# A gated product streamed through three SBUF slots: its DMA issues moved from SyncE to GpSimd, one packet per engine

## The chip, the cores and the metric

The kernel runs on one core of a Trainium2 chip. The metric is the device time of one execution in microseconds (us). Engines are named as in the profile: DVE is VectorE, ACT is ScalarE, POOL is GpSimd, SP is SyncE; a "q" behind a name (SPq) is the engine's instruction queue, in which waits and DMA issues are recorded. A core has 16 DMA engines, which move data between the chip's memory and SBUF.

## The reference

```python
def setup_inputs():
    return {"x": np.random.randn(8192, 8192).astype(np.float32)}

def reference(x):
    a, b = np.split(x, 2, axis=-1)
    silu_b = b / (1 + np.exp(-b))
    return a * silu_b
```

Each row of x has 8,192 floats. The first half is multiplied by the SiLU of the second half, which gives 4,096 floats. 268.4 MB are read and 134.2 MB written.

## The kernel before

The 8,192 rows are taken in 16 groups of 512. A group gives each of the 128 partitions four rows that follow one another in memory (R = 4). One group is loaded in two halves, `load(g, 0)` and `load(g, 1)`: two of the four rows, 64 KB per partition and 8.4 MB in all. The result of a group is four half rows per partition, again 64 KB, and is written by one `store(g)`. So there are 32 loads and 16 stores of the same size, 48 transfers in all.

There are three slots in SBUF of 64 KB per partition. For each group one slot is `keep` (it takes the first half and later holds the whole result) and one is `thru` (it takes the second half, which is read out of it). `swiglu(g, second, k0, k1)` works on rows k0 to k1 of a half: ScalarE replaces b by its SiLU in place (L72), VectorE multiplies a by it and writes the product into the `keep` slot (L74). The first half is done with one call of 2 x 4,096 elements per partition, the second with two calls of 4,096.

The slots change roles from group to group: the next group's `keep` is this group's `thru`, and its `thru` is the slot that the previous group's store empties. So the first load of the next group waits for the last product of this one, and the second load waits until the previous group's store has landed.

All 48 transfers are issued by one engine, SP, in an order written out by hand: three loads at the start; then after group 0 `load(1, 1)` and `store(0)`; after every later group g `load(g + 1, 0)`, `load(g + 1, 1)`, `store(g)`; and the last store alone. Issues are made in this order, so an issue that waits holds those behind it. Loads are issued at L61, stores at L81.

The schedule is manual: `behind` declares which waits an instruction needs and leaves out the others.

Of the kernel before, what the change touches and what calls it, by code (L numbers as in the profile page):

```python
# [1 line left out]

# [4 lines left out]

_SILU = mybir.ActivationFunctionType.Silu


@with_exitstack
def kernel(
    ctx: ExitStack,
    tc: tile.TileContext,
    x: bass.AP,
    out: bass.AP,
):

    nc = tc.nc
    N, M = x.shape
    half = M // 2
    P = nc.NUM_PARTITIONS
    R = 4
    ngroups = N // (P * R)

    xv = x.tensor.reshape([N // R, R * M]).ap()  # L30
    ov = out.tensor.reshape([N // R, R * half]).ap()

    pool = ctx.enter_context(tc.tile_pool(name="sbuf", bufs=1))
    ctx.enter_context(tc.manual_schedule())
    slots = [pool.tile([P, 2 * M], x.dtype, name=f"slot{s}") for s in range(3)]
    touched = [[] for _ in slots]
    newest = {}

    def behind(inst, of, *targets):


        for s in of:
            for t in touched[s]:
                if t not in targets and t is not newest.get(inst.ins.engine):
                    tc.declare_no_dep(inst.ins, t.ins, reason="ordered by the other waits")
        for s in of:
            touched[s].append(inst)
        newest[inst.ins.engine] = inst
        return inst

    keep, thru = [0, 2], [1, 1]
    for g in range(2, ngroups):
        keep.append(thru[g - 1])
        thru.append(keep[g - 2])
    free = {}
    landed = {}
    last = {}

    def load(g, second):
        s = (thru if second else keep)[g]  # L60
        inst = nc.sync.dma_start(  # L61
            out=slots[s], in_=xv[g * P : (g + 1) * P, second * 2 * M : (second + 1) * 2 * M]
        )
        behind(inst, [s], *([free[s]] if s in free else []))
        landed[g, second] = inst

    def swiglu(g, second, k0, k1):
        s, o = (thru if second else keep)[g], keep[g]
        rows = slots[s].rearrange("p (k s c) -> p k s c", k=2, s=2)
        a, b = rows[:, k0:k1, 0], rows[:, k0:k1, 1]  # L70
        to = slots[o].rearrange("p (k c) -> p k c", k=R)[:, 2 * second + k0 : 2 * second + k1]
        gate = nc.scalar.activation(out=b, in_=b, func=_SILU)  # L72
        behind(gate, [s], landed[g, second])
        prod = nc.vector.tensor_mul(out=to, in0=a, in1=b)  # L74
        behind(prod, {s, o}, gate, *([last[g]] if g in last else []))
        last[g] = prod
        free[s] = prod

    def store(g):
        s = keep[g]  # L80
        inst = nc.sync.dma_start(out=ov[g * P : (g + 1) * P], in_=slots[s])  # L81
        behind(inst, [s], last[g])
        free[s] = inst

    load(0, 0)
    load(0, 1)
    load(1, 0)
    for g in range(ngroups):
        swiglu(g, 0, 0, 2)
        for k in range(2):  # L90
            swiglu(g, 1, k, k + 1)
        if g == 0:
            load(1, 1)
            store(0)
        elif g + 1 < ngroups:
            load(g + 1, 0)
            load(g + 1, 1)
            store(g)
        else:
            store(g)  # L100


# [1 line left out]
_INS = ['x']  # L104
_OUTS = [((8192, 4096), 'float32')]


# [23 lines left out]
```

## Time and profile before

| | |
|---|---|
| median of 3 runs | 939.05 us (938.91 to 939.8) |
| the profiled execution: span, first to last instruction | 936.2 us |
| the profiled execution's own time | not recorded beside its span; the median of the runs is 2.85 us above the span |
| DVE busy | 279.2 us, 48 products |
| ACT busy | 227.7 us, 48 activations and a table load |
| POOL busy | 0.2 us, 4 MEMSETs |
| DMA | 402.67 MB, 430 GB/s on the mean, 6,912 packets in the data queue |
| DMA issues on SP | 32 loads of 0.33 us, 16 stores of 0.43 us (medians) |
| from issue to landing | loads 32.8 us, stores 57.7 us (medians) |

The span runs from the first to the last instruction of the profiled execution. Busy time of an engine counts its own work only; time in which a queue waits or issues a DMA is not in it. The time from issue to landing holds the time that a transfer waits behind earlier ones in the same DMA queue.

### The profile page before, as it was taken

The page shows a single profiled execution, that of the slowest core. Times are in us where ns is not written, and L with a number is a line of the kernel's source. Part 1 is how long each engine was busy: PE and PEld are TensorE (multiplying, and loading weights), DVE is VectorE, ACT ScalarE, POOL GpSimd, SP SyncE. Part 2 cuts the span into 40 slices and gives each one's busy share as a digit, 9 for nine tenths or more (in the row PEclk, how much of TensorE's full clock was granted, in tenths as well). Part 3 has the DMA queues.
Part 4 walks back from the last instruction along what each step waited for, and adds up shares of the span by engine and source line. Part 5 has one row for each costly group of instructions (what it writes and reads, how often), then busy time and mean ns, then how long its engine had stood idle before and what let it go on. Part 6 is the DMA issues. An engine that isn't in the chain of part 4 may idle for free.

```text
span 936.2 us, 235 instructions
## 1 busy us (share of the span) xinstructions
DVE 279.2 (30%) x48; ACT 227.7 (24%) x49; POOL 0.2 (0%) x4
## 2 busy tenths in 40 slices
DVE  0446033060330603316033160331503315033250
ACT  0433032330323303233032330413304133041330
POOL 0000000000000000000000000000000000000000
DMA  9999999999999999999999999999999999999997
GB/s 403 448 428 423 423 428 448 431 420 448 426 426 445 428 426 437 440 423 437 440 420 440 440 426 431 442 428 423 448 442 414 442 442 417 440 440 412 448 437 344
DMA packets 6914, 402.67 MB, mean 430 GB/s; under 512 B 768, under 2 KB 768, under 8 KB 768
## 3 DMA queue, kind: packets, MB, share of 16 engines
q1 hardware_dynamic: 6912, 402.66, 99.6%
q14 instruction: 2, 0.02, 0.0%
HBM read 268.44 MB, written 134.22 MB: 430 GB/s over the span
## 4 chain that ended last, share of the span: by engine, by line
DMA 67%; DVE 14%; another core or an unknown queue 9%; ACT 6%; SPq 1%; DVEq 0%; issue 0%
DMA slot<-in_x_dram 62%; DVE slot L74 14%; ACT slot L72 6%; DMA out_dram<-slot 5%; SPq L61 1%; DVEq L126 0%
## 5 line engine op out<-in xcount | busy, mean ns | idle before, releaser
L74 DVE TENSOR_TENSOR slot<-slot 128x4096 f32<-128x4096 f32 (+1 forms) x48 | 279.2, 5845 | 629.9 <-ACT slot L72 629.9
L72 ACT ACTIVATE slot<-slot 128x4096 f32<-128x4096 f32 (+1 forms) x48 | 226.4, 4748 | 675.5 <-DMA slot<-in_x_dram 675.5
L72 ACT ACT_TABLE_LOAD x1 | 1.3, 1283 | 0.7 <-PEq L115 0.7
L115 POOL MEMSET const-bfloat16-1.0<- 128x1 bf16 x1 | 0.1, 102 | 0.0
L115 POOL MEMSET const-uint8-127<- 128x1 uint8 x1 | 0.1, 102 | 0.0
L115 POOL MEMSET const-float32-0.0<- 128x1 f32 x1 | 0.1, 99 | 0.2 <-issue 0.2
L115 POOL MEMSET const-float32-1.0<- 128x1 f32 x1 | 0.1, 99 | 0.0
## 6 DMA issues: line engine op xcount, KB each, us to landing
slot<-in_x_dram SPq DMA_DIRECT2D x32, 32.8
out_dram<-slot SPq DMA_DIRECT2D x16, 57.7
```

The costliest lines, as they stand in the source:

```text
L61: inst = nc.sync.dma_start(out=slots[s], in_=xv[g * P : (g + 1) * P, second * 2 * M : (second + 1) * 2 * M])
L72: gate = nc.scalar.activation(out=b, in_=b, func=_SILU)
L74: prod = nc.vector.tensor_mul(out=to, in0=a, in1=b)
L115: nc = _bacc.Bacc("TRN2", target_bir_lowering=False, num_devices=1)
```

## The change

Loads and stores are issued on GpSimd's queue instead of SP's. The order of the issues and what each waits for are the same. Each issue is given `single_packet=True`, which asks that the part of a transfer that one DMA engine moves be framed as one packet, instead of a packet size chosen by the issuing code.

```diff
     def load(g, second):
         s = (thru if second else keep)[g]
-        inst = nc.sync.dma_start(
-            out=slots[s], in_=xv[g * P : (g + 1) * P, second * 2 * M : (second + 1) * 2 * M]
+        inst = nc.gpsimd.dma_start(
+            out=slots[s],
+            in_=xv[g * P : (g + 1) * P, second * 2 * M : (second + 1) * 2 * M],
+            single_packet=True,
         )
         behind(inst, [s], *([free[s]] if s in free else []))
         landed[g, second] = inst
...
     def store(g):
         s = keep[g]
-        inst = nc.sync.dma_start(out=ov[g * P : (g + 1) * P], in_=slots[s])
+        inst = nc.gpsimd.dma_start(out=ov[g * P : (g + 1) * P], in_=slots[s], single_packet=True)
         behind(inst, [s], last[g])
         free[s] = inst
```

## The prediction

> **What bounds the kernel now.** I read the page first: the span, the busy time of the engines and the row of the DMA engines.
>
> ```profile
> span 936.2 us, 235 instructions
> DVE 279.2 (30%) x48; ACT 227.7 (24%) x49; POOL 0.2 (0%) x4
> DMA  9999999999999999999999999999999999999997
> DMA packets 6914, 402.67 MB, mean 430 GB/s; under 512 B 768, under 2 KB 768, under 8 KB 768
> q1 hardware_dynamic: 6912, 402.66, 99.6%
> ```
>
> The compute engines are busy for less than a third of the span. The 16 DMA engines are busy in every slice, and one queue fills 99.6% of their time. So the time is the data divided by the pace of the DMA engines, plus what lies ahead of the first packet and behind the last one.
>
> The packet counts show how the data is cut. 48 transfers made 6,912 packets, which is 144 each, or 9 on each engine. 768 of them are tiny (16 for each transfer: the completion marks), and 6,144 carry data, 65,536 bytes each: one row of a slot. 0.996 x 16 x 936.2 us / 6,144 is 2.43 us for a data packet. The packet records behind these rows have a median of 2.418 us and a least of 2.415 us, and a tiny one takes less than 0.01 us. A transfer is 8 data packets deep on each engine, so 19.3 us.
>
> Next I read the queue's own waits, then the timeline of one group in the middle.
>
> ```profile
> SPq L61 <- DVE slot L74: 746.2, 15, 52.3
> SPq L61 <- DMA out_dram<-slot: 92.6, 14, 6.9
> SPq L81 <- DVE slot L74: 50.2, 1, 50.2
> ```
>
> ```profile
> 143.28 8.76 DVE L74 TENSOR_TENSOR slot<-slot 128x4096 f32<-128x4096 f32 x2 [7.24 <-ACT slot L72]
> 152.06 7.55 SPq L61 DMA_DIRECT2D slot<-in_x_dram  x2
> 159.66 0.42 SPq L81 DMA_DIRECT2D out_dram<-slot  x1
> 178.47 7.03 ACT L72 ACTIVATE slot<-slot 128x8192 f32<-128x8192 f32 x1 [31.72 <-DMA slot<-in_x_dram]
> 185.53 8.69 DVE L74 TENSOR_TENSOR slot<-slot 128x8192 f32<-128x8192 f32 x1 [33.49 <-ACT slot L72]
> 197.91 7.12 ACT L72 ACTIVATE slot<-slot 128x4096 f32<-128x4096 f32 x2 [12.42 <-DMA slot<-in_x_dram]
> ```
>
> The last product of a group ends at 152.0. SP issues the first load of the next group at once, then waits for the previous group's store to land, 92.6 / 14 = 6.6 us on the mean, issues the second load, and issues the store. While SP waits, the DMA engines still work on that older store. So the first load is in the queue 6.6 us before the engines reach it, the second load has the whole 19.3 us of the first ahead of it, and the store has more. The engines never run dry: a group takes (838.74 - 197.91) / 11 = 58.26 us between the starts of its first short ACTIVATE in the chain of waits, and 24 data packets in a row are 24 x 2.418 = 58.03 us. Only 0.23 us a group is something other than data at the usual pace.
>
> Last I read the two ends, in a table by windows (columns: window, length, then busy us of DVE, ACT, POOL, the clock, DMA share, GB/s).
>
> ```profile
> 0.00:1.00 1.00, 0.00 (x0) 0.28 (x1) 0.20 (x4) 1.00 0.00 0
> 1.00:1.70 0.70, 0.00 (x0) 0.70 (x1) 0.00 (x0) 1.00 0.00 0
> 1.70:3.00 1.30, 0.00 (x0) 0.31 (x1) 0.00 (x0) 1.00 2.43 807
> ```
>
> Nothing moves before 1.7 us, and SP's first issue starts at 0.73: 1.0 us from an issue to its first packet. At the other end SP sees the last store land at 935.4 and the span ends at 936.2.
>
> **The change, part by part.** The sum is made against the span of 936.2 us; the runs' median of 939.05 us is 2.85 us above it, and I carry that difference unchanged.
>
> The issuing instructions on SP (32 loads of 0.33 us, 16 stores of 0.43 us, 17.4 us in all) go away. Only the first of them lies on the path, since the others are issued while earlier transfers run. SP has nothing else to do, so what it stops doing is worth 0.
>
> The same 48 issues come to GpSimd's queue. In the profile before, that queue holds four MEMSETs of 0.1 us and the marks of the start and end, so the transfers get in front of nothing and stand behind nothing but that start. The two kinds of waits, for the last product and for the older store, go along. What is queued behind a waiting issue is again only the next transfer, in the same order as before, so the head-of-line behaviour is the same.
>
> What one issue costs on GpSimd no row shows: it never issues one here. For the 45 transfers after the start the cost is 0 as long as the cover holds: 6.6 us for the first load of each group, against 1.0 us from issue to packet on SP. GpSimd could be six times as slow and the engines would still find the load waiting. If it took more, each of the 15 groups would stop for the excess, and 0.13 us of excess would be enough to see (15 x 0.13 = 1.9 us, which is 0.2%, about what a measurement of this kernel can tell from no change).
>
> Whether VectorE is at work at these moments is in the timeline: after the last product it is idle for 33.49 us, and the three issues fall within the first 8. The first three issues of the program come before any product. The Trainium skill (SBUF — State Buffer, section "SBUF: two separate sides") warns that VectorE in a two-port mode locks GpSimd out of the port through which it writes descriptors, so that GpSimd's transfers start late. By that rule the sum would be the same here, because no issue falls beside a product.
>
> For the very first transfer there is no cover. The low end is SP's own 1.0 us, less 0.1 us because GpSimd sends the starting mark (0.61) and could pass it sooner: -0.1. The high end is twice SP's 1.0 us and one single-time load of the length of ScalarE's ACT_TABLE_LOAD, 1.28 us: +2.3. I take +0.8, nearer to the doubling of SP's row than to a load that nothing announces. All later work moves with it, since the engines are the limit from there on. The Trainium skill (DMA: Bandwidth & Descriptors, section "Specifications") gives about 1 us to the first byte for a GpSimd issue and 0.6 us for one of SP; by it the term would be an estimated +0.4 us and the sum 0.4 us lower. The trace has 1.0 us for SP.
>
> One packet per engine in place of eight changes where packets end, not how many bytes an engine moves. The median packet is 3 ns above the least one (2,418 against 2,415 ns): 3 ns x 384 data packets per engine is 1.2 us. The mean packet of 2.428 us stands 10 ns above the median, 3.6 us in all over 384; these are single packets of 2.5 to 3.3 us, mostly the first ones of a transfer. So merging can give at most 3.6 + 1.2 = 4.8 us, if both went; a loss has no bound in these rows and is a rival below. I take 0: engines that run back to back at one pace with a mark of under 0.01 us between transfers have little to save, and nothing says that the slow packets are slow for being packets.
>
> At the end, SP's drain after the last landing (7 ns) becomes one of GpSimd. GpSimd's drains in this trace take 34 to 181 ns, so 0 to +0.2, and I take +0.1.
>
> Sum: 0.8 + 0 + 0 + 0.1 = +0.9 us: a span of 937.1 us and a time of 940.0 us, 0.1% above before.
>
> **Rivals.**
>
> *A seam at every transfer (slower).* The engines may not pass from one GpSimd transfer to the next as smoothly as they do now, for instance if the mark of one large packet is awaited before the next packet begins. Its place is the 48 boundaries on each engine. Its price goes from 0 to the time a store's last packet needs to be known as landed: the last packet ends at 934.3 and SP sees it at 935.4, 1.1 us, so 48 x 1.1 = 53 us and 993 us in all. It decides from 0.04 us per transfer on (1.9 / 48, or from 0.02 if the start already takes 0.9). A middling 0.15 us gives 947. Against it: the marks are followed at once by the next data today, on the same engines. For it: nothing here shows the other way of issuing. Chance 0.22.
>
> *A late start (slower).* The first transfer takes 2 to 4 us more than on SP, because whatever GpSimd runs to make the packets is cold or long; the steady part is unchanged. That gives 941 to 943, with +3 as the middle: 942. For it: the start is the one place with no cover. Against it: the time is paid once. Chance 0.18.
>
> *The merged packets save (faster).* The slow first packets and the ends of packets shrink, up to 4.8 us, less the 0.9 of start and end: 935.2 at the most, 936.4 with three quarters of it. It needs 2.8 us of those 4.8 before it shows as over 0.2%. Against it: it needs both effects, more than half of each. Chance 0.13.
>
> *The flag does nothing.* A row of 65,536 bytes may stay a packet of its own whatever is asked. Since I gave the merging no gain, the time is 940.0 all the same; this lies within the forecast and only the packet count would tell.
>
> **How the numbers follow.** My forecast, a start that is a little later and all else covered, has 0.47: 940.0, and with its own bounds 938 to 940.9. That is the chance of within 0.2% (937.2 to 940.9). Late start and seam together make 0.40 for slower, and the merged packets 0.13 for faster. The range goes from 936.8, inside the gain of the merging, to 947, a seam of 0.15 us; I leave out some 0.08 below and 0.12 above, where a seam of the full price lies.
>
> **What would show it.** In the changed profile the queue of the data should be another than hardware_dynamic, with the DMA row at 9 in all slices. Right: the stretch without any packet at the start grows from 1.7 to about 2.5 us, a group still takes 58.2 to 58.3 us between its ACTIVATEs, and the older store still lands about 5 to 6 us after the last product. A seam shows as a longer group with fewer GB/s in every slice; a late start as empty windows before the first packet only; a saving as groups at or under 58.0 us. If the wait of the first load for its data begins right after its issue, with the engines empty, the cover of 6.6 us was not enough, and that step of mine is wrong.

## The result, and the profile after

The changed kernel takes 945.18 us (median of 4 runs, 942.72 to 946.1) against 939.25 us: a ratio of 1.0063, 95% interval [1.0051, 1.0075]. It is slower by 0.5 to 0.75%. The forecast was 940.0 us and "within 0.2%" as the likeliest case; the range reached to 947 and holds the time. The profiled execution took 945.11 us, of which its span is 943.3.

The page of the changed kernel, span, engines, DMA row and queues:

```profile
span 943.3 us, 235 instructions
DVE 279.2 (30%) x48; ACT 227.7 (24%) x49; POOL 25.7 (3%) x52
DMA  9999999999999999999999999999999999999997
q0 software_dynamic: 6912, 402.66, 99.3%
```

The compute engines do exactly the same work. The data has moved to another queue and is still 6,912 packets in the records: the records count the pieces of 64 KB whatever the flag asks. The DMA engines are busy in every slice as before. The packet records are finer than the slices: on the mean of the engines, the durations of the data packets add up to all but 1.3 us of the time from the first packet to the last (before: all but 1.1). So the loss can't be a stretch in which the engines wait for an issue. The waits of GpSimd's queue say the same (columns: us in total, times, longest):

```profile
POOL slot L61 <- DVE slot L76: 748.1, 15, 52.6
POOL slot L61 <- DMA out_dram<-slot: 90.4, 14, 6.9
```

And so does the timeline of a group:

```profile
203.19 8.76 DVE L76 TENSOR_TENSOR slot<-slot 128x4096 f32<-128x4096 f32 x2 [7.65 <-ACT slot L74]
212.24 0.53 POOL L61 DMA_DIRECT2D slot<-in_x_dram  x1 [50.10 <-DVE slot L76]
219.24 0.53 POOL L61 DMA_DIRECT2D slot<-in_x_dram  x1 [6.47 <-DMA out_dram<-slot]
```

An issue takes GpSimd 0.53 us, and after the first load of a group it waits 90.4 / 14 = 6.5 us until the older store lands (before: 6.6). The cover is still there.

Where the span grew by 7.1 us is read in three places. The first is the start, in the table by windows (columns as before):

```profile
1.00:1.70 0.70, 0.00 (x0) 0.70 (x1) 0.44 (x1) 1.00 0.00 0
1.70:2.60 0.90, 0.00 (x0) 0.31 (x1) 0.90 (x3) 1.00 0.00 0
2.60:3.00 0.40, 0.00 (x0) 0.00 (x0) 0.38 (x1) 1.00 6.98 2294
```

The first packet starts at 2.63 us; before it was 1.73. That is +0.9 us. (The share above 1 comes from packets that are counted in the window in which they start.) The issues stand in the two timelines, before and after:

```profile
0.73 53.92 SPq L61 DMA_DIRECT2D slot<-in_x_dram  x4
1.26 1.71 POOL L61 DMA_DIRECT2D slot<-in_x_dram  x3 [0.82 <-PEq L128]
```

So the 0.9 us has two parts. GpSimd's first issue starts 0.53 us later than SP's did (1.26 against 0.73), though GpSimd itself sends the starting mark at 0.61; the trace shows nothing on its queue between. From the start of the issue to the first packet it is 1.37 us, where SP took 1.00: +0.37.

The second place is the end, in the rows of the closing instructions (columns: shortest, median and longest duration in ns, first and last start in us):

```profile
L126 POOLq EVENT_SEMAPHORE  x4: 17/17/17, 935.6 to 936.1; - x4
L126 POOLq DRAIN  x3: 34/41/75, 0.7 to 936.0; - x3
L126 SPq DRAIN  x3: 7/7/7, 935.5 to 935.8; - x3
```

These are the rows before; after the change they are:

```profile
L128 POOLq EVENT_SEMAPHORE  x4: 17/17/17, 942.7 to 943.2; - x4
L128 POOLq DRAIN  x3: 45/89/27897, 914.7 to 943.1; - x3
L128 SPq DRAIN  x3: 7/7/7, 940.7 to 942.9; - x3
```

SP is through with its waits at 940.7. GpSimd's long DRAIN (one of the instructions that close the program) began at 914.7 and ends 27.9 us later, at 942.6: 1.9 us after SP. Only then comes GpSimd's mark (EVENT_SEMAPHORE, 942.7). Before, that mark stood at 935.6, within 0.03 us of the end of SP's DRAIN. From the last packet's end to the end of the span it is 1.2 us before and 3.1 us after: +1.9 us.

The third place is what lies between, from the first packet to the last. It grew from 933.3 to 937.6 us, by 4.4. In the chain of waits the start of the first short ACTIVATE of a group marks the pace of the stream, here before (L72) and after (L74):

```profile
197.91 3.62 ACT slot L72
838.74 3.63 ACT slot L72
199.54 3.62 ACT slot L74
843.99 3.63 ACT slot L74
```

(843.99 - 199.54) / 11 is 58.59 us a group, where it was 58.26. The packet records show where this is: the median packet is 2.418 us in both, but 242 packets are over it by more than 0.1 us where it was 122. Most of them are the eighth and last packet of a load that is followed by a store: 90 of the 122, and 171 of the 242. Added up per DMA engine, all excess over 2.418 us is 3.7 us before and 7.9 us after. These are one profiled execution each, and the excess differs between executions of one kernel, as the experiments show. I call the place of that last packet a passage from loads to stores; the kernel has 15 of them (the last two stores stand together).

### The profile page after: what moved, and what is told of

The parts are those of the page before. It is cut to its first block, busy times and chain, and to the rows that moved or that the text cites. A ratio compares the mean times of both kernels' runs of the same rounds, so it can differ in the third digit from the quotient of the medians.

```text
span 943.3 us, 235 instructions
## 1 busy us (share of the span) xinstructions
DVE 279.2 (30%) x48; ACT 227.7 (24%) x49; POOL 25.7 (3%) x52
## 3 DMA queue, kind: packets, MB, share of 16 engines
q0 software_dynamic: 6912, 402.66, 99.3%
## 4 chain that ended last, share of the span: by engine, by line
DMA 63%; DVE 13%; another core or an unknown queue 8%; issue 6%; ACT 5%; POOL 1%; POOLq 0%; PEldq 0%
DMA slot<-in_x_dram 58%; DVE slot L76 13%; ACT slot L74 5%; DMA out_dram<-slot 5%; POOL slot L61 1%; POOLq L128 0%; POOL out_dram L83 0%; PEldq L128 0%; POOLq L83 0%; POOLq L61 0%
## 5 line engine op out<-in xcount | busy, mean ns | idle before, releaser
L74 ACT ACTIVATE slot<-slot 128x4096 f32<-128x4096 f32 (+1 forms) x48 | 226.4, 4748 | 680.7 <-DMA slot<-in_x_dram 680.7
L61 POOL DMA_DIRECT2D slot<-in_x_dram x32 | 17.0, 532 | 839.3 <-DVE slot L76 748.1
L83 POOL DMA_DIRECT2D out_dram<-slot x16 | 8.6, 536 | 50.1 <-DVE slot L76 49.8
```

The source lines that it names most:

```text
L61: inst = nc.gpsimd.dma_start(out=slots[s], in_=xv[g * P : (g + 1) * P, second * 2 * M : (second + 1) * 2 * M], single_packet=True,)
L83: inst = nc.gpsimd.dma_start(out=ov[g * P : (g + 1) * P], in_=slots[s], single_packet=True)
```

## The experiments

Times are compared by medians, spans by the medians of the spans of all runs. The experiments were timed on four chips, always beside the kernel before; its medians there are 938.6 to 938.95 us. Outside the span lie 2.1 to 2.2 us (medians) in runs of the kernel before and 1.8 us in those of the changed one, so 0.4 us of what the span loses comes back there. It doesn't follow the issuer: other kernels that issue all on SP have 1.7 to 2.1 us there, and two on GpSimd have 2.05 and 2.08. Why it differs stays open.

**The changed kernel again** (no edit), beside the next two.

> The changed kernel as it is, timed beside the others on one chip. From the first result I expect a ratio to the kernel before of 1.005 to 1.0075 (+5 to +7 us). In its profile: first packet at about 2.6 us (before: 1.7), GpSimd's last DRAIN ending about 1.9 us after SP has seen the last store land, and the rest, 3 to 4.5 us, in data packets that take longer than 2.418 us, nearly all of them the last packet of a load that is followed by a store (before: 3.7 us of such excess per engine, after: 7.9 us).

Measured: 945.4 us against 938.89 us, ratio 1.0062 [1.005, 1.0075]. Its runs go from 942.98 to 945.97 us, those of the kernel before from 938.02 to 939.89. The profiled one was a short one (span 941.2): first packet 2.64 us, GpSimd 1.9 us behind SP at the end, excess 6.2 us. So start and end are the same in these two profiles, and it is the part between them that differs. Over all runs the span is 943.5 us against 936.8: start +0.9, end +1.9, between them +3.9.

**Without the flag.**

```diff
-            single_packet=True,
...
-        inst = nc.gpsimd.dma_start(out=ov[g * P : (g + 1) * P], in_=slots[s], single_packet=True)
+        inst = nc.gpsimd.dma_start(out=ov[g * P : (g + 1) * P], in_=slots[s])
```

> All transfers on GpSimd, without single_packet. Theory A (the loss belongs to the issue by GpSimd: start +0.9, end +1.9, the rest from how the engines pass between loads and stores, whatever the packets): within 1 us of the changed kernel, +5 to +7 us. Theory B (the loss between the ends belongs to the large packets): the excess of slow packets goes back to about 3.7 us per engine, and the time falls to +2.8 us, the two ends alone. Theory C (the flag saves something that the loss hides): slower than the changed kernel by 1 us or more.

Measured: 945.75 us, ratio 1.0077 [1.0064, 1.009], excess 8.3 us. Theory B falls: without the flag the loss is all there. Whether the flag saves a little can't be said from this pair, since the intervals of the two ratios overlap. A control with less spread follows below.

**First three loads and last store on SP, the rest as changed.**

```diff
+        if (g, second) in ((0, 0), (0, 1), (1, 0)):
+            inst = nc.sync.dma_start(out=slots[s], in_=src)
...
+        if g == ngroups - 1:
+            inst = nc.sync.dma_start(out=ov[g * P : (g + 1) * P], in_=slots[s])
```

> The changed kernel with its first three loads and its last store issued by SP, all else on GpSimd with single_packet. If start and end are what the trace says, first packet at 1.7 us again (-0.9 us) and no wait for GpSimd's DRAIN after the last landing (-1.9 us): 2.8 us less than the changed kernel, +2 to +4 us against the kernel before. If GpSimd's closing DRAIN costs its 1.9 us whenever there was a GpSimd transfer at all, only 0.9 us less. If the start of the stream doesn't set the end (the engines catch up), 1.9 us less.

Measured: 943.67 us, ratio 1.005 [1.0037, 1.0062], 1.7 us less than the changed kernel where 2.8 were expected; its runs spread from 941.19 to 945.91, so the time by itself proves little: the expected outcome in which the stream's start doesn't set its end (1.9 us less) is as near. The trace is plain about the places: the first packet starts at 1.75 us, and GpSimd's DRAIN no longer stands at the end.

```profile
L131 POOLq EVENT_SEMAPHORE  x4: 17/17/17, 938.4 to 939.3; - x4
L131 POOLq DRAIN  x3: 45/87/63930, 861.7 to 939.1; - x3
L131 SPq DRAIN  x3: 7/7/7, 938.3 to 938.6; - x3
```

The long DRAIN starts at 861.7 and is over at 925.6, while SP's store is still under way; SP's DRAIN at 938.3 is followed by GpSimd's mark at 938.4. So the DRAIN costs its 1.9 us only when it is the last thing waited for. From last packet to the end of the span it is 1.6 us here: 1.5 of the 1.9 us are back. Start and end together are 2.4 us shorter than in the changed kernel and the span by its medians 1.6 us (941.9 against 943.5), so the part between did not get shorter; a difference of this size lies within the spread of the runs.

**Loads sorted from stores, no compute.** The same bytes in 32 full loads and 32 stores of half the size out of one slot, on either engine.

```diff
+    def load_only(k):
+        s = 2 if k == 0 else k % 2
...
+        nc.sync.dma_start(out=slots[s], in_=src)
+
+    def store_half(k):
...
+        nc.sync.dma_start(out=dst, in_=slots[2][:, h * M : (h + 1) * M])
+
+    for k in range(2 * ngroups):
+        load_only(k)
+    for k in range(2 * ngroups):
+        store_half(k)
```

This is the version for SP, in place of the loop over the groups; the other has `nc.gpsimd.dma_start` with `single_packet=True`.

> A control without compute, all transfers on SP: the 32 loads one behind the other, then 32 stores of half the size out of one slot; the same bytes as before, one passage from loads to stores instead of 16. No SiLU, no product, the stores write raw data. Theory A (the loss between the ends lies in the passages from load to store): the excess over 2.418 us per packet falls from 3.7 us to about 1.5 us per engine (the first packet of all and the one passage), so about 2 us below the kernel before, 936 to 937.5 us. Theory B (it lies in every transfer, by issuer): no less excess per transfer than before, 938.5 to 939.5 us.

> The same control with all transfers on GpSimd, single_packet. Theory A: only start (+0.9) and end (+1.9, less 0.3 that lies outside the span) stand between this and its SP counterpart, so +2 to +3 us against it, with the same excess of slow packets, about 1.5 us. Theory B: besides these two ends 64 transfers cost at least what 48 cost in the changed kernel, +3 to +5 us more, so +6 us or more against its SP counterpart.

Measured: 934.80 us on SP, 4.1 us below the kernel before, with an excess of 1.9 us; 939.81 us on GpSimd, 5.0 us above SP. The runs differ less now (within 0.4 us on SP, 0.7 on GpSimd). On GpSimd the DRAIN again stands last:

```profile
L124 POOLq EVENT_SEMAPHORE  x4: 17/17/17, 937.4 to 938.0; - x4
L124 POOLq DRAIN  x3: 40/84/80273, 857.1 to 937.8; - x3
L124 SPq DRAIN  x3: 7/7/7, 934.8 to 937.7; - x3
```

It ends at 937.4, 2.5 us behind SP's DRAIN (the second of its three, at 934.9). It was 1.9 us after 48 GpSimd transfers and is 2.5 us after 64: 39 ns a transfer both times. Counted from the last landing of a GpSimd transfer to the end of this DRAIN, the traces have 2.2 us after 44 transfers (the kernel with its ends on SP), 2.3 to 2.4 us after 48 and 3.0 us after 64. So the end grows with the number of transfers, which I had not expected. From the first packet to the last there remain +1.5 us in the two traces, of which 0.6 are excess on the mean of the engines; besides, the 16 engines finish their last transfer within 1.8 us of each other, and within 0.3 us on SP. So neither theory has its figure: A expected +2 to +3, B +6 or more. The end took the extra 0.6 us, and the part between isn't zero with a single passage.

**Loads and stores in turn, no compute.**

```diff
+    load_only(0)
+    load_only(1)
+    for k in range(2 * ngroups):
+        store_half(k)
+        if k + 2 < 2 * ngroups:
+            load_only(k + 2)
```

> The control of the sorted kernels in another order, on SP: the same 64 transfers, but a load and a store of half the size in turn, 31 passages from load to store; no compute. Theory A: an excess of 0.1 to 0.2 us per passage as in the kernel before, so 3 to 6 us above its sorted counterpart. Theory B: the same as its sorted counterpart within 1 us.

> The same alternating order on GpSimd with single_packet. Theory A (passages cost more under GpSimd, 0.25 to 0.45 us each as in the changed kernel): 8 to 14 us above the sorted kernel on GpSimd, and the difference between GpSimd and SP is larger here than in the sorted pair by 3 to 8 us. Theory B: the difference between GpSimd and SP is the same in both pairs. Theory C (passages cost the same whoever issues; the changed kernel's surplus comes from compute beside the transfers): both alternating kernels stand equally far above their sorted ones.

Measured: 940.53 us on SP, 5.7 us above its sorted counterpart, and 946.70 us on GpSimd, 6.9 above. 30 more passages with the same transfers: 0.19 us each on SP, 0.23 on GpSimd (a passage here holds the turn back to the next load too). The excess in the two traces is 5.7 and 5.4 us per engine, and 4.8 and 4.6 us of it stand at the last packet of a load ahead of a store. So passages cost time; that is shown. That they cost twice as much under GpSimd, as theory A needs, is not: the difference between the engines grew by 1.2 us over 30 passages, not by 3 to 8.

**The order of the kernel, no compute.** Two loads, one store, the same 48 transfers.

```diff
-        behind(inst, [s], last[g])
+        behind(inst, [s])
...
-        swiglu(g, 0, 0, 2)
-        for k in range(2):
-            swiglu(g, 1, k, k + 1)
```

`behind` is emptied as well, so it leaves out no waits.

> The kernel before without SiLU and product: the same 48 transfers in the same order (two loads, one store), issued by SP, with waits on transfers alone, so that each issue comes some 19 us ahead of the engines instead of 6.6. The stores write raw data. If the time of before lies in the transfers and passages alone, it is 937 to 939.5 us, with 2.5 to 4 us of excess per engine over 2.418 us a packet.

> The same without compute on GpSimd with single_packet. Start, closing DRAIN and what lies outside the span give +2.6 us against its SP counterpart. Theory A (the surplus of some 4 us between the ends in the changed kernel comes from the order of the transfers and the issuer alone): +6 to +7 us against its SP counterpart, as in the full kernels. Theory C (that surplus needs the compute or the late issue beside it; the pairs without compute showed +1.4 to +2.8 us between the ends): +3.5 to +5 us.

Measured: 938.87 us on SP, the time of the full kernel (ratio to it 1.0003 [0.9994, 1.0012]). So on SP the compute costs nothing that shows. On GpSimd it is 943.64 us, ratio 1.005 [1.0036, 1.0064], 4.8 us above SP. By the spans, 941.6 against 937.1: start +0.9, end +2.0, between them +1.6. Theory C's range holds it. In the full kernel the part between is +3.9, so some 2.3 us of it come only with compute, or with the later issue that compute brings. From the spread of the runs I estimate that this difference is uncertain by some 1.2 us.

The excess of the slow packets does not follow the issuer in this pair. On SP it is 5.9 us in the profiled execution (a long one, span 938.6; 2.5 to 4 were expected), on GpSimd 4.1. From the first packet to the last these two executions take the same, 935.7 and 935.6 us, so the +1.6 rests on the medians of the spans alone. The traces of all kernels have an excess of 2.6 to 5.9 us on SP and 3.6 to 8.3 us on GpSimd, the sorted ones aside: one profile of each kernel can't tell which part of it belongs to the issuer.

**The flag by itself.** The sorted kernel on GpSimd without `single_packet`.

```diff
-        nc.gpsimd.dma_start(out=slots[s], in_=src, single_packet=True)
+        nc.gpsimd.dma_start(out=slots[s], in_=src)
...
-        nc.gpsimd.dma_start(out=dst, in_=slots[2][:, h * M : (h + 1) * M], single_packet=True)
+        nc.gpsimd.dma_start(out=dst, in_=slots[2][:, h * M : (h + 1) * M])
```

> The sorted kernel on GpSimd without single_packet: 32 loads, then 32 stores of half the size, no compute; this pair is quieter than the full kernels (0.7 us from lowest to highest), so it shows the flag by itself. If the flag saves time per transfer, this is slower than the 939.8 us of the flagged one, by 1 us or more over 64 transfers; if the flag does nothing, it is within 0.3 us; if long packets cost, it is faster.

Measured: 939.83 us (939.6 to 940.21) against 939.81 us with the flag. The two were timed on different chips; against the kernel before beside them the ratios are 1.0012 [1.0004, 1.0021] and 1.0006 [0.9998, 1.0015], which overlap, and both median spans are 938.1 us. Over 64 transfers the flag does nothing that can be measured, at pieces of 32 and 64 KB and in this order.

**Fewer passages in the full kernel, on SP.** Two groups are loaded, then two are stored, in the same three slots.

```diff
-    keep, thru = [0, 2], [1, 1]
-    for g in range(2, ngroups):
-        keep.append(thru[g - 1])
-        thru.append(keep[g - 2])
+    keep, thru = [], []
+    for g in range(0, ngroups, 2):
+        first, through = (0, 1) if g % 4 == 0 else (1, 0)
+        keep += [first, 2]
+        thru += [through, through]
...
-        if g == 0:
-            load(1, 1)
-            store(0)
-        elif g + 1 < ngroups:
-            load(g + 1, 0)
+        if g % 2 == 0:
             load(g + 1, 1)
             store(g)
         else:
             store(g)
+            if g + 1 < ngroups:
+                load(g + 1, 0)
+                load(g + 1, 1)
+                load(g + 2, 0)
```

> The full computation, all transfers on SP, with the order changed so that two groups are loaded and then two are stored: 8 passages from load to store instead of 16, same transfers, same three slots. By the passages (0.12 to 0.2 us each in the SP kernels) 1 to 1.6 us below the kernel before, 937.3 to 938 us, with an excess of 2 to 2.6 us per engine instead of 3.7. If the passages don't set the time, no change; if the new order lets the engines run dry anywhere (cover of 6.9 us by my count), slower.

Measured: 937.40 us against 938.65 us, ratio 0.9984 [0.9975, 0.9992], excess 2.6 us. Seven passages fewer (8 in place of 15) go with 1.25 us less. Of that, 0.4 us lies outside the span (1.7 us in place of 2.1 to 2.2). The span is 0.9 us shorter (935.7 against 936.6), which is 0.13 us a passage; the control had 0.19. This version is a little faster than both kernels of the case, and every DMA is issued by SP.

**Work beside the transfers.** The kernel without compute on GpSimd, with VectorE and ScalarE each busy on a tile of its own.

```diff
+    side = [pool.tile([P, 1024], x.dtype, name=f"side{k}") for k in range(2)]
...
+    for _ in range(700):
+        nc.scalar.activation(out=side[0], in_=side[0], func=_SILU)
+    for _ in range(700):
+        nc.vector.tensor_mul(out=side[1], in0=side[1], in1=side[1])
```

> The kernel without SiLU and product on GpSimd with single_packet, order two loads and one store, and beside it 700 activations and 700 products of 1,024 floats per partition on a tile of their own that no transfer waits for: VectorE and ScalarE busy for some 600 to 800 us, much more than the 30% of the full kernel. The transfers are issued early as in the kernel without compute. Without the side work it took 943.64 us. If it is the work of VectorE or ScalarE beside the transfers that lengthens the changed kernel's packets by about 2 us, 945.5 us or more, with an excess per engine of 6 us or more. If it is the late issue (6 us ahead of the engines), 943 to 944.3 us and an excess of about 4 us, as without the side work.

Measured: 945.38 us (944.97 to 945.58), 1.7 us more than without the side work. From the page:

```profile
DVE 859.7 (91%) x702; ACT 741.1 (79%) x701; POOL 25.7 (3%) x52
q14 instruction: 12, 0.10, 0.0%
L52 POOL DMA_DIRECT2D slot<-in_x_dram x32 | 17.0, 532 | 837.9 <-DMA slot<-in_x_dram 573.1
```

The time came close to what the theory of the work beside expects, but not by the way it names: the excess of slow packets is 3.6 us, no more than the 4.1 us without. What grew is the distance between the first and the last of the 16 engines to finish a transfer, 7.7 us at the end of the stream in place of 5.4 us (3.6 and 3.2 us in the kernels before and after). And the side work was three times that of the full kernel.

The trace offers another account, which the expectation did not name. The 1,400 added instructions bring DMA traffic of their own: the row q14 counts 12 packets of instructions, 8 KB and 0.31 to 0.47 us each, on the same DMA engines (the kernel without side work has none during its stream). When each engine's packets are put in order, one beginning where the one before ended, six of the 12 fall on one engine, five of them beyond doubt, and it is the one that finishes last. They take 2.0 us of its time (the five 1.7 us), as much as the kernel lost. Without them it would be done at 937.7 us, no later than the last engine without side work (938.2). So it isn't shown that work on VectorE or ScalarE slows GpSimd's transfers; the loss here can be the fetching of the side work's instructions. The full kernels have two or three such packets in the whole span, on different engines. The two kernels were also timed on different chips. The late issue alone was not tried.

## Why the prediction was right or wrong

The range was right and the likeliest case was not: the kernel is slower by more than 0.2%, which had 0.40. That the range holds the time is owed to the room it left for a seam, not to the sum: the sum has +0.9 us for the span, and the spans grew by 6.7 us (start +0.9, end +1.9, between them +3.9, where +0.8, +0.1 and 0 were taken). Of the 6.7 us, 0.4 came back outside the span. Point by point:

- *What bounds the kernel.* Right. The DMA engines bound it before and after, and the kernel without compute takes the same time on SP (938.87 us).
- *The moved issues and their cover.* Right. The second load's wait is 6.5 us where it was 6.6, the three issues take 0.53 us each, and no group stops for them. One sign was set wrong: the older store was to land 5 to 6 us after the last product, but the prediction's own rows have 7.2 us (152.04 to 159.28), and after the change it is 7.3 (211.95 to 219.24).
- *VectorE and the rule on its port.* The forecast that it changes nothing in this order held: after the first, GpSimd's issues take 527 to 538 ns each. They take no longer with VectorE 91% busy beside them. The Trainium skill (SBUF — State Buffer, "SBUF: two separate sides") ties the lock-out to a two-port mode of VectorE. No view here tells in which mode the products run, so that rule itself is not tested.
- *The start.* +0.8 us was taken, +0.9 us measured, in every kernel whose first load GpSimd issues (2.63 to 2.66 us to the first packet). The figure is right by luck. The working doubled SP's 1.0 us from issue to packet, which on GpSimd is 1.37, and let GpSimd begin up to 0.1 us sooner, where it began 0.53 us later. The Trainium skill's first-byte figures (DMA: Bandwidth & Descriptors, "Specifications") made an estimated +0.4 us. From issue to packet the traces agree with that difference (+0.37 us), though not with the figures themselves (1.00 and 1.37 us against 0.6 and 1). The later start of the first issue is not in them.
- *The end.* A term mis-sized: +0.1 us, at most +0.2, was taken from short drains of GpSimd when it had issued no transfer. It measured +1.9 us, and about 39 ns more for each further transfer issued. A row of the same name under other conditions was no bound.
- *The packets.* Merging gained nothing that shows (939.81 against 939.83 us), as "I take 0" had it. But the step took 0 for the whole part between the ends, and there it failed: +3.9 us over all runs. In the profiled executions the excess of slow packets went from 3.7 to 7.9 us per engine. The prediction saw the slow packets as "mostly the first ones of a transfer" and put them at 2.5 to 3.3 us; the records of the same trace have 90 of 122 at the last packet of a load ahead of a store, and up to 3.7 us.
- *The rival of the seam.* Its price of 0.04 us or more per transfer is near what came, 3.9 / 48 = 0.08, and its chance was 0.22. The sign that it had named came too: a group takes 58.59 us, where the forecast had 58.2 to 58.3. Its place was not: seven in ten of the slow packets stand at passages from load to store, not at all 48 boundaries. The controls with a single passage still have +1.5 us between the ends, 0.02 us a transfer. Its highest price rests on a misreading: the last packet ends at 935.0, not 934.3, and SP sees it 0.4 us later, not 1.1. That makes 19 us and 959 us in all, not 53 and 993; the range and the middling 0.15 us don't use it.
- *The 2.85 us outside the span.* The kernel's other runs have 2.1 to 2.2 us there on the median. The rest of the 2.85 would be a profiled execution some 0.7 us shorter than the median; its own time is not on record. Carried unchanged, the 2.85 us hid 1 us of what the span's sum was short of, since the changed kernel has 1.8.

What stays open is the larger half of the loss: why the part between the ends grows at all when GpSimd issues (+1.6 us without compute), and whether it truly grows more with compute (+3.9 us). The flag is not the cause (the loss is there without it), and the engines don't wait for an issue (the cover held).

## What to carry to other kernels

When the DMA engines are busy from end to end, look at what no cover hides: the time to the first packet, what the closing instructions wait for, and how often the stream turns from loads to stores. Moving issues to another engine left the bytes as they were and cost 6 us, 2.8 us of span at the start and the end and the rest between them; asking for larger packets gave nothing where the pieces were 64 KB already. Ordering the same transfers so that they turn half as often went with 1.25 us less, 0.9 us of it in the span. And look at what an experiment adds besides what it is meant to add: instructions have to be fetched too.

## What the runs showed of the hardware

- A passage from loads to stores in one queue costs 0.13 us (full kernel, by the spans) to 0.19 us (control) on SP and 0.23 us on GpSimd (control), at 8.4 MB loads.
- GpSimd's closing DRAIN ends 1.9 us after SP's when GpSimd issued 48 transfers, 2.5 us with 64, and was over before the end (925.6 of 939.4 us) when a store of SP landed last.
- A full-size load or store takes GpSimd 0.53 us to issue (SP: 0.33 to 0.43), and the first packet of the program starts 0.9 us later than from SP: 0.5 us because the first issue starts later, 0.4 us more from issue to packet.
- A transfer issued by GpSimd with single_packet leaves records of the same 64 KB pieces as one of SP, at the same 2.418 us each.
- Instruction packets of 8 KB run on the same 16 DMA engines as the data and take 0.31 to 0.47 us each; six fell on one engine in the kernel with 1,400 side instructions.
